# More paired slabs in the feed-forward part, with the down combinations rebuilt from reloaded tiles and adding DMAs

## Chip, cores and metric

The kernel runs on one core of a Trainium2 chip. The metric is the device time of one execution in microseconds (us). Data and results are fp32; every large product is made of three fp32r matmuls (high x high, high x low, low x high parts), so each weight tile and each feature tile is split into a rounded high part and the rest, its low part.

## The reference, cut to what matters

One encoder layer for 256 rows of width 2048. Mixers and cross-attention come first; the change touches only the last part, the feed-forward block.

```
def swiglu(h, w_gate_up, w_down):
    gate, up = jnp.split(h @ w_gate_up, 2, axis=-1)
    return (jax.nn.silu(gate) * up) @ w_down
...
        x = x + swiglu(rms_norm(x, norm_g[l, 2]), w_gate_up[l], w_down[l])
    return rms_norm(x, final_norm_g)
```

`w_gate_up` is 2048 x 11264, `w_down` is 5632 x 2048. The 256 rows are two row blocks of 128.

## The kernel before

**The stream of weights.** All weights lie in one array of slabs of 128 x 2048 (16 blocks of 128 x 128, in the order of use). A slab is loaded by SyncE (SP) into a `raw` buffer. `Stream._half` splits it in halves of 1024 columns: ScalarE (ACT) casts to `wh` (L135), VectorE (DVE) subtracts to `wl` (L136). Four `wh`/`wl` buffers of each kind exist in this part (three, and one of `st.extra`), and `_fill` makes halves ahead as far as they reach. TensorE (PE) takes a half and runs, for each 512 columns and each row block, the three matmuls of `part` (L433, L434, L435; L441 to L443 after the change). A plain slab, "N" in the plans, is 8 such products, 24 matmuls.

**Paired slabs.** A slab marked "S" holds a 2 x 2 set of weight blocks: two feature tiles (`ks`) by two column blocks of 512. With two row blocks it is a product of 2 x 2 block matrices, made with 7 products instead of 8 (Strassen-Winograd), 21 matmuls. It needs sums of weight blocks, which `Stream._sums` makes in four phases of 1024, 512, 1024 and 1024 columns. In the third phase DVE adds 512 columns four times (L157); if the slab is also in `SUMMED`, a DMA that adds (`two`, L102, issued by GpSimd, POOL) has done part of this, and DVE adds twice. Each phase is cast (L159) and subtracted (L160) as above. It also needs combinations of feature tiles, which `combine` makes into a `z` or `y` tile: sums of high and low parts, four sums of 128 columns, then `split2` (L299 on ACT, L283 on DVE) for the high and low parts. In down the fourth piece, x4, goes to half of the first feature's own tile. `forms` names the pieces. The products come in the order 1, b0 (with x4), a0, two of 5 and 7, a1, 6.

**Gate and up.** 11 groups of 512 columns. The first has no pairs. Each of the other ten takes 8 slabs by the plan `GROUP` with 3 S, whose combinations of the 16 features are made once and used in all groups. At the end of a group `mixed`, `gated` and `upped` combine the PSUM banks on DVE and ACT (L1067, L1077), `up` multiplies, transposes (L557) and stores the group's four feature tiles to the `hidden` array (L559, POOL).

**Down.** 44 feature tiles f (k = 0 to 43) by 2048 columns, in two passes of 1024 columns, 22 slabs each by `PASSES`. `fetch` reloads hidden tiles turned (`load_turned`, L564, POOL) and splits them (L291, L283): 22 during gate and up, 22 (`FT - 22` on) at the start of down. Pass 0 begins with four N, which use the features without pairs. `before(j)` makes a combination by hand, if it isn't there yet, when its S comes. Three slabs of the last columns stay for `down_end`, which adds a split of a combined part by a product with the identity (L1244), then the held products of row block 0 and its norm, then of row block 1.

**What sets the order.** `Background` is a list of generators that are stepped between matmuls, by a clock of the program's own (`bg.now`, about one us of PE each) and an account of work that DVE owes. A `yield n` means: not before n us later. `keep_place(mark)` ties each instruction since the mark to the one ahead of it on its engine; where it isn't used, the scheduler of the tile framework may move instructions on their engine. Each engine runs its own in order.

Of the kernel before, what the change touches and what calls it, by code (L numbers as in the profile page):

```python
# [13 lines left out]
F32 = mybir.dt.float32  # L14
F32R = mybir.dt.float32r
# [4 lines left out]
ALU = mybir.AluOpType  # L20
# [3 lines left out]
P = 128  # L24
R = 256
D = 2048
KT = D // P
DFF = 5632
# [15 lines left out]
GATE_UP = 1920 // 16 + 8  # L44
GROUP = "NNSNSNSN"

DOWN = GATE_UP + 80
PASSES = "NNNNSNNSNNSNNSNNSNNSNN", "NSNSNSNSNSNSNSNSNSNNNN"

PAIRED = {a + i for a, plan in [(GATE_UP + 8 * j, GROUP) for j in range(10)] + [(DOWN, PASSES[0]), (DOWN + 22, PASSES[1])]  # L50
          for i, x in enumerate(plan) if x == "S"}
SUMMED = {i for i in PAIRED if i < DOWN}

LAG, OWED, SOON, FAR = 1.3, 0.9, 0.01, 18.0
# [200 lines left out]
class Block:  # L255
# [25 lines left out]
    def tt(self, out, a, b, op):  # L281
        self.bg.dve(math.prod(out.shape[1:]))
        self.nc.vector.tensor_tensor(out=out, in0=a, in1=b, op=op)  # L283
# [14 lines left out]
    def split2(self, hi, lo, src):  # L298
        self.nc.scalar.copy(hi, src)  # L299
        self.tt(lo, src, hi.bitcast(F32), ALU.subtract)  # L300

    def gap(self, pool, n):

        pool.tile([P, n // 4], F32, name=f"gap{next(self.kept)}")
# [132 lines left out]

    def combine(self, z, a, b):

        tt, t, u, v, w = self.tt, *(self.tmp() for _ in range(4))  # L440
        for x, y in ((t, a), (u, b)):  # L441
            tt(x, y[:, 0:R].bitcast(F32), y[:, R:512].bitcast(F32), ALU.add)
        yield SOON  # L443
        tt(v[:, 0:P], t[:, P:R], u[:, P:R], ALU.subtract)
        tt(w[:, 0:P], t[:, 0:P], t[:, P:R], ALU.subtract)
        tt(v[:, P:R], v[:, 0:P], t[:, 0:P], ALU.subtract)
        tt(w[:, P:R], u[:, 0:P], v[:, P:R], ALU.add)
        yield SOON
        hi, lo, x4 = self.forms(z, a)
        self.split2(hi[:, 0:R], lo[:, 0:R], v)  # L450
        if hi.shape[1] == 512:
            self.split2(hi[:, R:512], lo[:, R:512], w)
        else:
            self.split2(hi[:, R:], lo[:, R:], w[:, 0:P])
            self.split2(*x4, w[:, P:R])

# [7 lines left out]
    def paired_rows(self, w, cols, slots, sums, plan, mixed, first, ready=None, late=0, before=None, swap=False):  # L464
# [12 lines left out]
        def put(name, hi, lo, wh, wl):  # L477
            if name not in q:
                for x in [name] if name in count else "1675":
                    q[x] = (self.bank if (name in count) == swap else self.gbank)()  # L480
                    left[x] = count.get(x, s)
            new = left[name] == count.get(name, s)
            left[name] -= 1
            self.part(q[name][:, :], hi, lo, wh, wl, new, left[name] == 0)

        form = lambda t, r: (t[:, r * P:(r + 1) * P], t[:, R + r * P:R + (r + 1) * P])
        n = done = 0
        for i, kind in enumerate(plan):
            if before:
                before(i)  # L490
            if kind == "S":
                ks, z = next(todo)
# [554 lines left out]
    def gate_up(self, gp, f, z):  # L1047
# [39 lines left out]
        def fetch(k0, k1, ahead, pause, wait=0):  # L1087

            m = {}
            for k in range(k0, k1 + ahead):  # L1090
                if k < k1:
                    while len(stored) <= k // 4:
                        yield
                    m[k] = self.tmp()
                    self.load_turned(m[k], self.ff, k)
                if k >= k0 + ahead:
                    while wait and self.bg.now < stored[(k - ahead) // 4] + wait:
                        yield
                    mark = self.mark()
                    self.split(f[k - ahead], m.pop(k - ahead))  # L1100
                    self.keep_place(mark)
                    self.have = k - ahead + 1
                    yield pause
# [18 lines left out]

        sums = [((2 * i, 2 * i + 1), z[i]) for i in range(GROUP.count("S"))]
        comb = self.bg.add(combined())
# [8 lines left out]
        for j in range(1, DFF // 512):  # L1133
            upped(j, self.paired_rows("w_gate_up", [j * 512, DFF + j * 512], self.h3, sums, GROUP, mixed, gated, swap=j % 2 == 0)[0])
        self.bg.drain(early)
        self.fetch = self.bg.add(fetch(FT - 22, FT, 6, SOON))

    def down(self, f, sp):
# [72 lines left out]
    def down_end(self, f, ss, ps, rest, split):  # L1211
# [28 lines left out]

        mark = self.mark()
        for j, parts in split:
            for a in parts:
                nc.tensor.matmul(ps[1][:, j:j + R], self.identr, a, start=False, stop=False)  # L1244
        self.keep_place(mark)
        held = [(k, *st.take("w_down", k, 3 * 512, 4)) for k in rest]
# [644 lines left out]
```

## Time and profile before

| | |
|---|---|
| three runs | 1436.64, 1436.71, 1439.13 us (median 1436.71) |
| profiled execution | 1435.07 us, of it the span from first to last instruction 1433.3 us |
| granted TensorE clock, mean | 0.999 |
| PE, DVE, ACT, POOL busy | 99%, 80%, 57%, 16% |
| DMA, mean over the span | 240 GB/s |

Gate and up with pairs begin near 780 us, down near 1193 us. A row of a timeline has start, length, engine, line, operation, tiles written and read, and in brackets the engine's idle time before it with what ended it. A row of the groups has the count, busy us and mean ns of one, then idle time. The rows themselves are shown where the prediction uses them.

### The profile page before, as it was taken

To read this page: it belongs to the slowest core of one execution; us is meant where nothing else is said; L and a number is where in the kernel's file an instruction comes from. 1 tells how busy PE (TensorE), PEld (TensorE's weight loads), DVE (VectorE), ACT (ScalarE), POOL (GpSimd) and SP (SyncE) were. 2 spreads that over 40 slices of the span, in tenths; PEclk is the share of its full clock that TensorE was granted. 3 is DMA by queue.
4 is the path that set the end of the run, shared out by engine and by line. 5 is a ranking of instruction groups with operands and counts; after the bars stand their busy time and mean duration, and the time that the engine had idled before them with its cause. 6 is when DMAs were issued, how large, how long until landed. Compare 5 with 4: busy or idle time off the path is not lost.

```text
span 1433.3 us, 18652 instructions
## 1 busy us (share of the span) xinstructions
PE 1423.0 (99%) x6589; PEld 1180.7 (82%) x6589; DVE 1146.2 (80%) x1738; ACT 815.2 (57%) x1183; POOL 234.8 (16%) x306
## 2 busy tenths in 40 slices
PE   9999999999999999999999999999999999999997
PEld 8888888888888888888888888888888888888886
DVE  6667868777877767777677888898888888989997
ACT  7556565446645555556554656555555556655655
POOL 0000100013212223531431121122011002000000
PEclk9999999999999999999999999999999999999999
DMA  9876564546667788964986999889999887655554
GB/s 352 299 285 248 205 206 162 175 169 224 202 196 236 234 267 252 274 200 166 289 239 209 286 286 277 278 275 282 294 293 288 268 260 229 219 230 179 193 218 147
DMA packets 73037, 343.79 MB, mean 240 GB/s; under 512 B 10957, under 2 KB 12654, under 8 KB 45168
## 3 DMA queue, kind: packets, MB, share of 16 engines
q1 hardware_dynamic: 54848, 288.98, 57.5%
q0 software_dynamic: 17664, 52.97, 15.8%
q8 instruction: 51, 0.84, 0.2%
q10 hardware_dynamic: 432, 0.66, 0.1%
q14 instruction: 42, 0.34, 0.1%
HBM read 322.12 MB, written 20.45 MB: 239 GB/s over the span
## 4 chain that ended last, share of the span: by engine, by line
PE 97%; DVE 1%; ACT 0%; DMA 0%; issue 0%; SPq 0%; ACTq 0%
PE pg L433 22%; PE pg L434 22%; PE pg L435 22%; PE pm L434 7%; PE pm L435 7%; PE pm L433 7%; PE pg L381 4%; PE pg L382 2%; PE pm L1344 1%; PE pm L1022 1%; PE pm L993 1%; DMA raw<-in_W 0%; PE pm L1753 0%; DVE res L283 0%; PE pm L994 0%
## 5 line engine op out<-in xcount | busy, mean ns | idle before, releaser
L136 DVE TENSOR_TENSOR wl<-raw,wh 128x1024 fp32r<-128x1024 f32 (+1 forms) x413 | 494.8, 1212 | 166.1 <-ACT wh L135 163.2
L135 ACT CAST wh<-raw 128x1024 fp32r<-128x1024 f32 (+1 forms) x413 | 424.5, 1043 | 283.9 <-PE pg L435 196.4
L433 PE MATMUL pg<-wh,act 128*128 128x512 f32 (+1 forms) x1191 | 465.6, 391 | 0.0
L434 PE MATMUL pg<-wl,act 128*128 128x512 f32 (+1 forms) x1191 | 463.9, 389 | 0.4 <-DVE wl L136 0.2
L435 PE MATMUL pg<-wh,act 128*128 128x512 f32 (+1 forms) x1191 | 463.9, 389 | 0.0
L433 PEld LDWEIGHTS pg<-wh,act 128*128 128x128 f32 x1191 | 223.8, 188 | 47.8 <-issue 1.5
L434 PEld LDWEIGHTS pg<-wl,act 128*128 128x128 f32 x1191 | 223.8, 188 | 47.2 <-DVE wl L136 1.3
L435 PEld LDWEIGHTS pg<-wh,act 128*128 128x128 f32 x1191 | 223.7, 188 | 47.2 <-DVE act L283 0.4
L159 ACT CAST wh<-raw 128x1024 fp32r<-128x1024 f32 (+1 forms) x150 | 137.0, 921 | 146.8 <-DVE raw L157 46.4
L160 DVE TENSOR_TENSOR wl<-raw,wh 128x1024 fp32r<-128x1024 f32 (+1 forms) x150 | 156.1, 1061 | 57.0 <-ACT wh L159 56.8
L434 PE MATMUL pm<-wl,act 128*128 128x512 f32 x309 | 120.5, 390 | 0.1
L433 PE MATMUL pm<-wh,act 128*128 128x512 f32 x309 | 120.2, 389 | 0.0
L435 PE MATMUL pm<-wh,act 128*128 128x512 f32 x309 | 120.2, 389 | 0.0
L381 PE MATMUL pg<-act,wh 128*128 128x512 f32 x256 | 90.5, 395 | 0.0
L382 PE MATMUL pg<-act,wl 128*128 128x256 f32 x256 | 71.8, 280 | 0.0
L434 PEld LDWEIGHTS pm<-wl,act 128*128 128x128 f32 x309 | 58.0, 188 | 13.0 <-DVE wl L136 0.6
L433 PEld LDWEIGHTS pm<-wh,act 128*128 128x128 f32 x309 | 58.0, 188 | 12.0
L435 PEld LDWEIGHTS pm<-wh,act 128*128 128x128 f32 x309 | 58.0, 188 | 12.0
L102 POOL DMA_DIRECT2D two<-in_W x30 | 26.6, 887 | 241.2 <-DMA two<-in_W 116.0
L157 DVE TENSOR_TENSOR raw<-raw 128x512 f32<-128x512 f32 x90 | 62.0, 689 | 1.3
L159 ACT CAST wh<-two 128x1024 fp32r<-128x1024 f32 x30 | 31.6, 1052 | 51.1 <-PE pg L435 21.7
L381 PEld LDWEIGHTS pg<-act,wh 128*128 128x128 f32 x256 | 48.1, 188 | 10.5
(375 smaller groups left out, 1821.9 us busy)
## 6 DMA issues: line engine op xcount, KB each, us to landing
raw<-in_W SPq DMA_DIRECT2D x216, 1024.0 KB, 5.6
raw<-in_W SPq DMA_DIRECT2D x30, 768.0 KB, 6.1
two<-in_W SPq DMA_DIRECT2D x60, 256.0 KB, 4.9
two<-in_W POOLq DMA_DIRECT2D x30, 512.0 KB, 9.3
raw<-in_W SPq DMA_DIRECT2D x11, 512.0 KB, 7.6
hidden<-g POOLq DMA_DIRECT2D x22, 256.0 KB, 3.7
tmp<-hidden POOLq DMA_DIRECT2D x44, 128.0 KB, 5.4
features<-tmp POOLq DMA_DIRECT2D x32, 128.0 KB, 5.3
```

The costliest lines, as they stand in the source:

```text
L102: nc.gpsimd.dma_start(t, W[:, 512:1536], accum_op=ALU.add)
L135: nc.scalar.copy(wh[:, a:b], r[:, a:b])
L136: nc.vector.tensor_tensor(out=wl[:, a:b], in0=r[:, a:b], in1=wh[:, a:b].bitcast(F32), op=ALU.subtract)
L157: nc.vector.tensor_tensor(out=out, in0=a, in1=b, op=ALU.add)
L159: nc.scalar.copy(wh, src)
L160: nc.vector.tensor_tensor(out=wl, in0=src, in1=wh.bitcast(F32), op=ALU.subtract)
L381: self.nc.tensor.matmul(p[:, :], wh, slot[:, :], start=start, stop=False)
L382: self.nc.tensor.matmul(p[:, 0:R], wl, slot[:, 0:R], start=False, stop=stop)
L433: self.nc.tensor.matmul(p, hi, wh, start=start, stop=False)
L434: self.nc.tensor.matmul(p, hi, wl, start=False, stop=False)
L435: self.nc.tensor.matmul(p, lo, wh, start=False, stop=stop)
L993: nc.tensor.matmul(p[:, :], q[d][:, r * P:(r + 1) * P], kt[d][:, :], start=d == 0, stop=False)
```

## The change

1. `GROUPS` replaces `GROUP`: every second gate and up group has the plan "NSNSsNSN". Its fourth pair uses a new tile z3; "s" is paired, but not summed by DMA.
2. The down plans have 8 and 10 S in place of 6 and 9.
3. A down combination (`src` given) loads the two features again from `hidden`, in place of adding their high and low parts, and yields 8, 4 and 6 us.
4. `split_far`: the high part by a cast (L305 of the new kernel), the low part as the negated source, written by ACT (L306) to fp32r, to which a DMA from POOL adds the source (L308). It is used in the down combinations and for the last 22 features.
5. `put` keeps the place of its matmuls.
6. The identity products of `down_end` move behind row block 0's held products and norm.

```
-GROUP = "NNSNSNSN"
+GROUPS = "NNSNSNSN", "NSNSsNSN"
...
-PASSES = "NNNNSNNSNNSNNSNNSNNSNN", "NSNSNSNSNSNSNSNSNSNNNN"
+PASSES = "NNNNSNSNSNNSNSNSNNSNSN", "NSNSNSNSSNSNSNSNSSNNNN"
...
+    def split_far(self, hi, lo, src):
+
+        mark = self.mark()
+        self.nc.scalar.copy(hi, src)
+        self.nc.scalar.mul(lo, src, -1.0)
+        self.keep_place(mark)
+        self.nc.gpsimd.dma_start(lo, src, accum_op=ALU.add)
...
-    def combine(self, z, a, b):
+    def combine(self, z, a, b, src=None):
 
         tt, t, u, v, w = self.tt, *(self.tmp() for _ in range(4))
-        for x, y in ((t, a), (u, b)):
-            tt(x, y[:, 0:R].bitcast(F32), y[:, R:512].bitcast(F32), ALU.add)
-        yield SOON
+        if src:
+            for x, k in zip((t, u), src):
+                self.load_turned(x, self.ff, k)
+            yield 8.0
+        else:
+            for x, y in ((t, a), (u, b)):
+                tt(x, y[:, 0:R].bitcast(F32), y[:, R:512].bitcast(F32), ALU.add)
+            yield SOON
...
-        yield SOON
+        yield 4.0 if src else SOON
         hi, lo, x4 = self.forms(z, a)
-        self.split2(hi[:, 0:R], lo[:, 0:R], v)
+        split = self.split_far if src else self.split2
+        split(hi[:, 0:R], lo[:, 0:R], v)
...
+            mark = self.mark()
             self.part(q[name][:, :], hi, lo, wh, wl, new, left[name] == 0)
+            self.keep_place(mark)
...
-                    self.split(f[k - ahead], m.pop(k - ahead))
-                    self.keep_place(mark)
+                    t, x = f[k - ahead], m.pop(k - ahead)
+                    if k0:
+                        self.split_far(t[:, 0:R], t[:, R:512], x)
+                    else:
+                        self.split(t, x)
+                        self.keep_place(mark)
...
-                yield from self.combine(x, *(f[k] for k in ks))
+                yield from self.combine(x, *(f[k] for k in ks), ks)
+                yield 6.0
                 made.append(x)
-                yield 2.0
...
-        mark = self.mark()
-        for j, parts in split:
-            for a in parts:
-                nc.tensor.matmul(ps[1][:, j:j + R], self.identr, a, start=False, stop=False)
-        self.keep_place(mark)
...
         for r in range(2):
+            mark = self.mark()
+            for j, parts in split if r else ():
+                for a in parts:
+                    nc.tensor.matmul(ps[1][:, j:j + R], self.identr, a, start=False, stop=False)
             for k, wh, wl in held:
                 self.part_rows(ps[r], r, f[k], wh, wl, False, k == FT - 1)
+            self.keep_place(mark)
             norm(ps[r], r)
```

More of the change, by code (lines that the diff above doesn't have):

```diff
@@ L44 @@
 GATE_UP = 1920 // 16 + 8
-GROUP = "NNSNSNSN"
+GROUPS = "NNSNSNSN", "NSNSsNSN"
 DOWN = GATE_UP + 80
-PASSES = "NNNNSNNSNNSNNSNNSNNSNN", "NSNSNSNSNSNSNSNSNSNNNN"
-PAIRED = {a + i for a, plan in [(GATE_UP + 8 * j, GROUP) for j in range(10)] + [(DOWN, PASSES[0]), (DOWN + 22, PASSES[1])]
-          for i, x in enumerate(plan) if x == "S"}
-SUMMED = {i for i in PAIRED if i < DOWN}
+PASSES = "NNNNSNSNSNNSNSNSNNSNSN", "NSNSNSNSSNSNSNSNSSNNNN"
+PAIRED = {a + i for a, plan in [(GATE_UP + 8 * j, GROUPS[j % len(GROUPS)]) for j in range(10)] + [(DOWN, PASSES[0]), (DOWN + 22, PASSES[1])]
+          for i, x in enumerate(plan) if x in "Ss"}
+SUMMED = {GATE_UP + 8 * j + i for j in range(10) for i, x in enumerate(GROUPS[j % len(GROUPS)]) if x == "S"}
 LAG, OWED, SOON, FAR = 1.3, 0.9, 0.01, 18.0
@@ L447, in combine @@
         tt(w[:, P:R], u[:, 0:P], v[:, P:R], ALU.add)
-        yield SOON
+        yield 4.0 if src else SOON
         hi, lo, x4 = self.forms(z, a)
-        self.split2(hi[:, 0:R], lo[:, 0:R], v)
+        split = self.split_far if src else self.split2
+        split(hi[:, 0:R], lo[:, 0:R], v)
         if hi.shape[1] == 512:
-            self.split2(hi[:, R:512], lo[:, R:512], w)
+            split(hi[:, R:512], lo[:, R:512], w)
         else:
-            self.split2(hi[:, R:], lo[:, R:], w[:, 0:P])
-            self.split2(*x4, w[:, P:R])
+            split(hi[:, R:], lo[:, R:], w[:, 0:P])
+            split(*x4, w[:, P:R])
     def forms(self, z, a):
@@ L490, in paired_rows @@
                 before(i)
-            if kind == "S":
+            if kind in "Ss":
                 ks, z = next(todo)
@@ L1121, in combined @@
                 yield from self.combine(z, *(self.h3[k] for k in ks))
-        sums = [((2 * i, 2 * i + 1), z[i]) for i in range(GROUP.count("S"))]
+        z = z + [gp.tile([P, 1024], F32R, name="z3")]
+        sums = [((2 * i, 2 * i + 1), z[i]) for i in range(4)]
         comb = self.bg.add(combined())
@@ L1133, in gate_up @@
         for j in range(1, DFF // 512):
-            upped(j, self.paired_rows("w_gate_up", [j * 512, DFF + j * 512], self.h3, sums, GROUP, mixed, gated, swap=j % 2 == 0)[0])
+            plan = GROUPS[(j - 1) % len(GROUPS)]
+            upped(j, self.paired_rows("w_gate_up", [j * 512, DFF + j * 512], self.h3, sums[:8 - plan.count("N")], plan, mixed, gated,
+                                      swap=j % 2 == 0)[0])
         self.bg.drain(early)
```

## The prediction

> **What bounds the kernel now.** I read the page first: the span, the busy shares and the chain that ended last.
>
> ```profile
> span 1433.3 us, 18652 instructions
> ...
> PE 1423.0 (99%) x6589; PEld 1180.7 (82%) x6589; DVE 1146.2 (80%) x1738; ACT 815.2 (57%) x1183; POOL 234.8 (16%) x306
> ...
> PE 97%; DVE 1%; ACT 0%; DMA 0%; issue 0%; SPq 0%; ACTq 0%
> ```
>
> TensorE (PE) is the chain: 97% of it. Removing a matmul shortens the kernel, as long as everything that feeds PE still comes in time. What a matmul is worth is not the 0.39 us that a record lasts, since records overlap; it is the step from one start to the next. From the timeline of PE, the first and the last of a run of 60 matmuls that follow each other:
>
> ```profile
> 1179.71 0.39 PE L434 MATMUL pm<-wl,act 128*128 128x512 f32 x1
> ...
> 1193.08 0.39 PE L433 MATMUL pg<-wh,f 128*128 128x512 f32 x1
> ```
>
> 13.37 us over 59 steps: 0.2267 us each. So a plain slab ("N", 24 matmuls) is 5.44 us of PE and a paired slab ("S", 21) is 4.76 us.
>
> Then I asked how near the other engines are, stretch by stretch (columns: PE, PEld, DVE, ACT, POOL busy, clock, DMA share, GB/s):
>
> ```profile
> 800.00:900.00 100.00, 100.00 (x443) 82.84 (x442) 87.32 (x103) 58.28 (x70) 17.24 (x20) 1.00 0.95 287
> 1200.00:1300.00 100.00, 99.97 (x439) 81.53 (x438) 91.05 (x150) 59.94 (x91) 11.46 (x13) 1.00 0.64 218
> ```
>
> VectorE (DVE) has 87% in the gate and up part and 91% in the down part. It is the second bound, and an S slab is dearer for it than an N slab. So the question is whether DVE and the new DMAs keep PE fed.
>
> The prices, from the groups by form and from the DMA issues (us from issue to landing, last column):
>
> ```profile
> L136 DVE TENSOR_TENSOR wl<-raw,wh 128x1024 fp32r<-128x1024 f32 x408 | 492.0, 1220 | 163.5 <-ACT wh L135 160.6
> L157 DVE TENSOR_TENSOR raw<-raw 128x512 f32<-128x512 f32 x90 | 62.0, 689 | 1.3
> L160 DVE TENSOR_TENSOR wl<-raw,wh 128x512 fp32r<-128x512 f32 x45 | 30.8, 685 | 0.3 <-ACT wh L159 0.3
> L283 DVE TENSOR_TENSOR z<-tmp,z 128x256 fp32r<-128x256 f32 x12 | 4.8, 419 | 0.0
> L299 ACT CAST y<-tmp 128x256 fp32r<-128x256 f32 x9 | 3.6, 403 | 6.3 <-DVE tmp L283 6.3
> L299 ACT CAST y<-tmp 128x128 fp32r<-128x128 f32 x9 | 2.7, 295 | 2.4 <-DVE tmp L283 2.4
> L787 ACT ACTIVATE tmp<-res 128x256 f32<-128x256 f32 x8 | 3.1, 420 | 2.7 <-DVE res L283 2.7
> L564 POOL DMA_DIRECT2D tmp<-hidden x44 | 38.8, 889 | 53.7 <-issue 24.4 <-DMA hidden<-g 13.3 <-DVE act L283 10.0
> L918 POOL DMA_DIRECT2D mr<-values x16 | 8.8, 552 | 30.4 <-DVE kt L283 20.3 <-DVE tmp L1007 9.8 <-issue 0.2
> ```
>
> ```profile
> two<-in_W POOLq DMA_DIRECT2D x30, 512.0 KB, 9.3
> tmp<-hidden POOLq DMA_DIRECT2D x44, 128.0 KB, 5.4
> values<-tmp POOLq DMA_DIRECT2D x16, 128.0 KB, 2.2
> mr<-values POOLq DMA_DIRECT2D x16, 128.0 KB, 3.4
> ```
>
> **What it removes.** Five gate and up groups get a fourth S, pass 0 of down goes from 6 to 8, pass 1 from 9 to 10: 8 S in place of N, 3 matmuls each, 24 x 0.2267 = 5.4 us of PE. On DVE a down combination loses two sums and its three low parts, and 22 late features lose theirs (0.42 us for 128x256). That DVE time was hidden beside PE and is worth nothing by itself.
>
> **The fourth S of the gate and up groups.** An N costs DVE two subtractions of 1.22 = 2.4 us. The new S ("s") is not summed by DMA: three subtractions of 1.22, one of 0.69, four sums of 0.69 = 7.1 us, beside 4.76 us of PE. By the window, a group of 41.5 us (5 N and 3 S) has 0.873 x 41.5 = 36.2 us of DVE; with s in place of an N it is 40.9, and PE's time falls to 40.8. On average DVE is then full in every second group, so each unevenness inside such a group ends on PE. Two places are uneven.
>
> First, the group's opening. The DVE work that ends the group before runs into the next one; from the timeline, DVE and below it the PE matmuls that first use a half:
>
> ```profile
> 860.75 1.22 DVE L136 TENSOR_TENSOR wl<-raw,wh 128x1024 fp32r<-128x1024 f32 x1
> ...
> 865.00 1.30 DVE L557 STREAM_TRANSPOSE g<-h 128x512 f32<-128x512 f32 x2
> 866.23 1.18 DVE L136 TENSOR_TENSOR wl<-raw,wh 128x1024 fp32r<-128x1024 f32 x1
> ```
>
> ```profile
> 867.68 0.39 PE L434 MATMUL pg<-wl,act 128*128 128x512 f32 x1
> 868.36 0.39 PE L434 MATMUL pg<-wl,act 128*128 128x512 f32 x1
> ...
> 869.72 0.39 PE L434 MATMUL pg<-wl,act 128*128 128x512 f32 x1
> ```
>
> Here DVE is free of the old group at 866.23, with an N on PE. In the changed plan ("NS...") an S stands there, and its second, third and fourth phases are first used at 867.68, 868.36 and 869.72. DVE still has to do from 866.23 on: 512 subtraction, sum, 1024 subtraction (third phase, ready at 868.65: 0.3 late), sum, a subtraction of the next N that the built program's order puts ahead, then the fourth phase, ready at 871.6: 1.55 later still. 1.85 us in all.
>
> Second, s follows an S directly. An unsummed S between N slabs, in the down part of before:
>
> ```profile
> 1330.34 1.82 DVE L160 TENSOR_TENSOR wl<-raw,wh 128x1024 fp32r<-128x1024 f32 x2
> ...
> 1335.36 1.22 DVE L160 TENSOR_TENSOR wl<-raw,wh 128x1024 fp32r<-128x1024 f32 x1
> ...
> 1338.26 2.36 DVE L136 TENSOR_TENSOR wl<-raw,wh 128x1024 fp32r<-128x1024 f32 x2
> ```
>
> ```profile
> 1335.80 0.39 PE L434 MATMUL pg<-wl,act 128*128 128x512 f32 x1
> ...
> 1337.84 0.39 PE L434 MATMUL pg<-wl,y 128*128 128x512 f32 x1
> ...
> 1340.56 0.39 PE L434 MATMUL pm<-wl,act 128*128 128x512 f32 x1
> ```
>
> Its first phase is ready 4.2 us ahead (1331.6 for 1335.80) and four sums eat that down to 1.3 us (1336.58 for 1337.84). But whatever follows an S starts only 1.08 us ahead (1339.48 for 1340.56). So s loses 3.1 us of lead, less some 0.7 us of small work that stood between: it is late by about 1.0 us in the third phase, and 0.95 more in the fourth, again behind a subtraction of the next N. 1.95 us. The new z3 is made once, in the first group, which has no S to feed; it costs nothing. Five groups: 5 x 3.8 = 19.0 us. I bound this at 9 us (half) and 28 us (half as much again). In down the same happens at the first adjacent pair of pass 1 (1.95 us), and pass 1 starts one N nearer to the work that ends pass 0 (about 2.4 us, by the same walk): 4.4 us.
>
> **The low parts by DMA.** Before, a combination's low part was one DVE instruction. Now it is a cast and a negation on ScalarE (ACT), an issue on POOL and a landing, three times for each S of down, and the piece that is first needed (x4) is issued last. Two things fix it late. All ten combinations are issued by hand against the S that uses them; with the new 8, 4 and 6 us pauses one takes some 19 us of the program's own clock, and S slabs come every 10 to 16. And both ACT's split and PE's matmuls now hold their order, so PE can't go on with another product. In the built program's order ACT's six instructions stand behind the cast for the third phase of the very S. How late that cast is, from before, with the start of its S below:
>
> ```profile
> 1228.26 1.05 ACT L159 CAST wh<-raw 128x1024 fp32r<-128x1024 f32 x1 [1.78 <-DVE raw L157]
> ```
>
> ```profile
> 1230.48 0.39 PE L433 MATMUL pm<-wh,act 128*128 128x512 f32 x1
> ```
>
> It ends 1.2 us before S; with less DVE work it can come about 0.5 earlier, no more, since it needs a buffer that PE frees. Six instructions (0.40, 0.42, then four of about 0.30, overlapping a little) take 1.9 us: the last ends near S + 0.25. The first use of x4's low part is PE's sixth matmul, S + 1.1. No row shows an accumulation of 64 or 128 KB inside SBUF. Its landing lies between 2.0 us (a little under values<-tmp) and 5.4 (tmp<-hidden); two<-in_W accumulates, but four times the bytes. I take 3.4, from mr<-values, the same shape into SBUF. Landing at S + 3.65: 2.5 us of waiting for each of six S, 15 us.
>
> The other four are worse. At the first S of pass 0 the adds too stand at its door, behind the subtraction of its own fourth phase, which ends near S + 2.6; adds to 3.2, ACT to 5.3, landing 8.7, needed at 1.1: 7.6 us. (POOL is full by then: 16 low parts of 0.55, 13 loads of 0.89 and two stores since the start of down, some 22 us of issues in the 21.8 us that PE takes to the first S.) At the second and third the split stands among those of the features, and a load or a low part goes ahead on POOL: last issue near S + 2.1 and 1.8, waits of 4.4 and 4.1. The last of pass 1 follows another S directly and its split starts near S + 1.4, behind a cast: 5.6. Four features (act 22, 23, 2, 3) are issued some 3 us before use, landing included 0.4 late each: 1.5. Sum 15 + 21.7 + 1.5 = 38 us. With 2.0 for the landing, ten waits are 1.4 shorter and the features don't wait: 22. With 5.4, ten are 2.0 longer and four features 1.0: 62.
>
> [...]
>
> **The end.** The identity matmuls now stand behind row block 0's held products; before, PE's weight loads waited there for the split parts:
>
> ```profile
> 1410.47 0.19 PEld L1244 LDWEIGHTS pm<-tmp,identr 128*128 128x128 f32 x1 [0.20 <-ACT tmp L299]
> ...
> 1410.93 0.19 PEld L1244 LDWEIGHTS pm<-tmp,identr 128*128 128x128 f32 x1 [0.27 <-DVE tmp L283]
> ```
>
> I count these 0.4 us as gained.
>
> **Sum**, on the profiled execution (span 1433.3, time 1435.07; the median of the three runs is 1.64 higher): -5.4 + 19.0 + 4.4 + 38 - 0.4 = +55.6, so 1490.7 there and 1492 as a median.
>
> **Rivals.** (a) The forecast: DVE and DMA both hold PE, 1492; 0.50. (b) The low parts land in time and only DVE is late: -5.4 + 23.4 - 0.4, 1454. For it: the 2.2 us row. Against: even that lands after S + 1.1. 0.12. (c) Only the DMAs cost, because DVE has idle time ahead of each tight place: -5.4 + 38 - 0.4, 1469. For it: before shows leads of 1 us held without loss. Against: that lead is just what s uses up. 0.18. (d) Faster: the split reaches POOL early enough, the other 5.4 us are gained, 1431. That needs ACT to start the six instructions 3 us earlier than now (the last issue by S - 2.3), and DVE to lose none of its leads; one step on the wrong side and it's gone. 0.04, and 0.02 for no change. (e) The waits cost more than themselves, because PE's clock falls after them. The trace shows such a fall behind the last matmul (clock: the third column from the right):
>
> ```profile
> 1428.00:1430.00 2.00, 0.00 (x0) 0.00 (x0) 0.00 (x0) 0.00 (x0) 0.00 (x0) 0.83 1.03 377
> 1430.00:1433.00 3.00, 0.00 (x0) 0.00 (x0) 0.00 (x0) 0.00 (x0) 0.00 (x0) 0.50 0.22 74
> ```
>
> ```profile
> 1424.47 0.24 PE pm L435
> ```
>
> The last row is the last matmul, from the chain. 0.83 is 0.68 us at half clock in 2: the clock fell at 1429.3, some 4.5 us after the last matmul. Two of my waits are longer, two as long. If half clock lasts another 4.5 us, each costs 2.2 us more: 4 to 9 us, 1496 to 1501; with landings of 5.4 us nearly every S would do it, up to 1535. 0.14. [...]
>
> **Numbers.** About 0.2% is what a measurement of this kernel can tell from no change. Faster 0.04, same 0.02, slower 0.94. The range holds (a), (b), (c) and most of (e): 1452 to 1522.
>
> **What would show it.** PE's timeline should have steps of 2 to 6 us inside each S of down, on the third matmul of the second product (act, then f), released by a DMA; in every second gate and up group two steps of 0.5 to 1.6 us, released by DVE. DVE's share in 800 to 1100 us should rise above 90%, and POOL should be full for some 20 us at the start of down. If PE's steps stay at 0.23 us throughout, I am wrong; if only one of the two kinds shows, (b) or (c) holds.

## The result and the profile after

The changed kernel takes 1561.46 us (median of five runs, 1556.29 to 1563.36) against 1436.64 (1435.42 to 1439.13): 1.0863 times as long, 95% interval 1.084 to 1.0885. It is slower, as forecast, but by 125 us and not by 56; 1561 lies outside the range of 1452 to 1522.

The page of the changed kernel: span, busy shares, and the chain that ended last.

```profile
span 1559.1 us, 18804 instructions
...
PE 1459.1 (94%) x6565; PEld 1191.8 (76%) x6565; DVE 1169.5 (75%) x1731; ACT 845.6 (54%) x1256; POOL 300.1 (19%) x378
...
issue 10%; PE 3%; DVE 2%; POOL 2%; DMA 1%; ACT 0%; POOLq 0%; DVEq 0%
```

24 matmuls fewer (6565 against 6589), and yet 36 us more PE busy time: records last longer, above all where the clock is halved (0.63 us each in the rows of S 5 below, against 0.39). The chain that was 97% PE is broken, so it can't be used for shares any more. What tells are PE's groups with idle time ahead of them (line, engine, operation, tiles, count; busy, mean ns; idle before, and what ended it). L441, L442 and L443 are a product's first, second and third matmul (hi by wh, hi by wl, lo by wh):

```profile
L441 PE MATMUL pg<-wh,act 128*128 128x512 f32 (+1 forms) x1196 | 469.7, 393 | 5.4 <-ACT act L305 5.4
L443 PE MATMUL pg<-wh,act 128*128 128x512 f32 (+1 forms) x1196 | 469.4, 393 | 25.9 <-DMA act<-tmp 25.9
...
L442 PE MATMUL pm<-wl,act 128*128 128x512 f32 x279 | 111.3, 399 | 10.9 <-DVE wl L160 10.9
...
L442 PE MATMUL pg<-wl,z 128*128 128x512 f32 x99 | 41.3, 417 | 7.7 <-DVE wl L160 7.7
L443 PE MATMUL pg<-wh,z 128*128 128x512 f32 x99 | 41.1, 415 | 12.0 <-DMA z<-tmp 12.0
...
L443 PE MATMUL pg<-wh,f 128*128 128x512 f32 x42 | 18.5, 441 | 10.5 <-DMA f<-tmp 10.5
...
L443 PE MATMUL pm<-wh,f 128*128 128x512 f32 x30 | 13.0, 432 | 9.6 <-DMA f<-tmp 9.6
```

25.9 + 12.0 + 10.5 + 9.6 = 58.0 us of waiting on the adding DMAs, all at the third matmul, the one that reads a low part; z here is also the tile of the first late features. The second matmul, which reads a weight's low half, waits on VectorE (DVE).

One S of pass 0, the fifth, shows all of it. First POOL's timeline, then PE's (start, duration, engine, line; idle before it in brackets):

```profile
1351.60 1.72 POOL L308 DMA_DIRECT2D y<-tmp  x2 [10.72 <-ACT y L306]
1352.67 1.52 POOL L308 DMA_DIRECT2D f<-tmp  x1
```

```profile
1355.75 0.79 PE L443 MATMUL pg<-wh,f 128*128 128x512 f32 x1 [2.82 <-DMA f<-tmp]
1356.34 0.63 PE L441 MATMUL pg<-wh,f 128*128 128x512 f32 x1
1356.77 0.63 PE L442 MATMUL pg<-wl,f 128*128 128x512 f32 x1
1357.19 0.63 PE L443 MATMUL pg<-wh,f 128*128 128x512 f32 x1
1357.62 0.63 PE L441 MATMUL pm<-wh,y 128*128 128x512 f32 x1
1358.05 0.63 PE L442 MATMUL pm<-wl,y 128*128 128x512 f32 x1
```

POOL idles until ACT has split the pieces, issues the two of y and last the one that PE needs first; PE idles 2.82 us; and behind that its starts lie 0.427 us apart and not 0.227. PE's clock does fall between matmuls: 0.50 was granted from 1355.2 to 1358.5 us. "Half clock" below means such steps.

From PE's timeline of 817 us on I summed, over all matmuls, the step from the start before less 0.2267 us. Steps over 0.62 us are waits, those of 0.40 to 0.62 are put down as half clock:

| place | forecast, us | measured, us |
|---|---|---|
| gate and up | 19.0 | 35.0 |
| four late features, on their DMA | 1.5 | 17.6 |
| S 1 to 3 of pass 0 | 7.6 + 4.4 + 4.1 | 7.8 + 8.7 + 8.2 |
| S 4 to 8 of pass 0 | 5 x 2.5 | 2.6, 3.0, 2.7, 2.5, 2.9 |
| S 9 and 10 | 2.5 + 5.6 | 6.7 + 6.2 |
| pass 1, opening and adjacent pair | 4.4 | 3.9 |
| end | -0.4 | 1.1 |
| half clock in down | 0 (rival e: 4 to 9) | 22.0 |
| small steps in down | 0 | 2.6 |

The right column adds up to 133.5; less the 1.8 that before has in the same stretch and less 5.4 for the matmuls, it is 126.3, and the spans differ by 125.8. Not every wait is one for DVE or for a DMA. Of the 35.0 in gate and up, 22.9 are waits for DVE's weight halves, 3.3 waits for ACT's casts of them, and 8.8 steps below 0.62 us, short waits and half clock. In S 1, 2 and 10, 4.1, 1.6 and 3.0 us are waits for ACT's cast of x4; the first expectations below counted the 4.1 with the features.

The table says where PE lost time, not yet what would give it back. That took the experiments.

### The profile page after: what moved, and what is told of

The parts are those of the page before. It is cut to its first block, busy times and chain, and to the rows that moved or that the text cites. A ratio compares the mean times of both kernels' runs of the same rounds, so it can differ in the third digit from the quotient of the medians.

```text
span 1559.1 us, 18804 instructions
## 1 busy us (share of the span) xinstructions
PE 1459.1 (94%) x6565; PEld 1191.8 (76%) x6565; DVE 1169.5 (75%) x1731; ACT 845.6 (54%) x1256; POOL 300.1 (19%) x378
## 5 line engine op out<-in xcount | busy, mean ns | idle before, releaser
L136 DVE TENSOR_TENSOR wl<-raw,wh 128x1024 fp32r<-128x1024 f32 (+1 forms) x397 | 477.0, 1212 | 196.1 <-ACT wh L135 194.0
L135 ACT CAST wh<-raw 128x1024 fp32r<-128x1024 f32 (+1 forms) x397 | 409.7, 1042 | 329.7 <-PE pg L443 204.1
L443 PE MATMUL pg<-wh,act 128*128 128x512 f32 (+1 forms) x1196 | 469.4, 393 | 25.9 <-DMA act<-tmp 25.9
L441 PE MATMUL pg<-wh,act 128*128 128x512 f32 (+1 forms) x1196 | 469.7, 393 | 5.4 <-ACT act L305 5.4
L442 PE MATMUL pg<-wl,act 128*128 128x512 f32 (+1 forms) x1196 | 468.0, 391 | 0.0
L443 PEld LDWEIGHTS pg<-wh,act 128*128 128x128 f32 x1196 | 226.1, 189 | 76.5 <-DMA act<-tmp 29.1
L159 ACT CAST wh<-raw 128x1024 fp32r<-128x1024 f32 (+1 forms) x182 | 167.0, 923 | 197.5 <-PE pg L443 78.3
L441 PEld LDWEIGHTS pg<-wh,act 128*128 128x128 f32 x1196 | 226.3, 189 | 53.9 <-ACT act L305 6.3
L442 PEld LDWEIGHTS pg<-wl,act 128*128 128x128 f32 x1196 | 226.1, 189 | 47.3 <-DVE wl L136 1.0
L160 DVE TENSOR_TENSOR wl<-raw,wh 128x1024 fp32r<-128x1024 f32 (+1 forms) x182 | 190.3, 1064 | 82.8 <-ACT wh L159 82.7
L442 PE MATMUL pm<-wl,act 128*128 128x512 f32 x279 | 111.3, 399 | 10.9 <-DVE wl L160 10.9
L441 PE MATMUL pm<-wh,act 128*128 128x512 f32 x279 | 110.2, 395 | 1.3 <-ACT wh L159 1.3
L443 PE MATMUL pm<-wh,act 128*128 128x512 f32 x279 | 109.7, 393 | 0.0
L157 DVE TENSOR_TENSOR raw<-raw 128x512 f32<-128x512 f32 x122 | 84.0, 689 | 2.6
L580 POOL DMA_DIRECT2D tmp<-hidden x64 | 69.1, 1129 | 86.1 <-DVE f L283 16.2
L442 PEld LDWEIGHTS pm<-wl,act 128*128 128x128 f32 x279 | 53.0, 190 | 27.3 <-DVE wl L160 16.2
L441 PEld LDWEIGHTS pm<-wh,act 128*128 128x128 f32 x279 | 53.0, 190 | 14.6 <-ACT wh L159 3.5
L443 PEld LDWEIGHTS pm<-wh,act 128*128 128x128 f32 x279 | 53.0, 190 | 10.7
L159 ACT CAST wh<-two 128x1024 fp32r<-128x1024 f32 x30 | 31.4, 1047 | 49.4 <-PE pg L443 27.2
```

The costliest lines, as they stand in the source:

```text
L135: nc.scalar.copy(wh[:, a:b], r[:, a:b])
L136: nc.vector.tensor_tensor(out=wl[:, a:b], in0=r[:, a:b], in1=wh[:, a:b].bitcast(F32), op=ALU.subtract)
L157: nc.vector.tensor_tensor(out=out, in0=a, in1=b, op=ALU.add)
L159: nc.scalar.copy(wh, src)
L160: nc.vector.tensor_tensor(out=wl, in0=src, in1=wh.bitcast(F32), op=ALU.subtract)
L441: self.nc.tensor.matmul(p, hi, wh, start=start, stop=False)
```

## The experiments

Unless said otherwise the comparisons are of three rounds beside runs of the kernel before on the same chip; "saves" is against 1561.5. The kernel before had medians of 1436.2 to 1437.7 in these rounds, so a difference of 2 us between two versions says little.

**All low parts on DVE.**

```
     def split_far(self, hi, lo, src):
...
-        self.nc.scalar.copy(hi, src)
-        self.nc.scalar.mul(lo, src, -1.0)
...
-        self.nc.gpsimd.dma_start(lo, src, accum_op=ALU.add)
+        self.split2(hi, lo, src)
```

> All of the change, but every low part is again one subtraction on VectorE (cast, then subtract) in place of a cast, a negation and an adding DMA. In the changed kernel's trace PE's steps above 0.2267 us in the down part add up so: 21.7 us at the first features, 34.3 at the S slabs of pass 0, 12.9 at the last two S slabs of pass 1, and 22.1 of matmuls at half clock behind these. Theory A (the adding DMAs cause all of that): 1561.5 - 91.0 = 1470. Theory B (VectorE is so full that the low parts, put back on it, are late themselves; 18 combinations of 0.8 us and 22 features of 0.42 us are 24 us of VectorE): 1480 to 1495.

1481.8 us, ratio 1.0311 (1.0296 to 1.0326). It saves 79.7: the adding DMAs are the larger cause. The time lies in theory B's range, at its lower end, but not quite for B's reason: PE's waits in down, 13.7 us with the end's, are all for weight halves, from DVE or from ACT's casts of them, and none is for a low part of a feature or of a combination.

**Old gate and up plan.**

```
-GROUPS = "NNSNSNSN", "NSNSsNSN"
+GROUPS = "NNSNSNSN", "NNSNSNSN"
```

> All of the change but the fourth pair: every gate and up group keeps the plan NNSNSNSN. In the changed kernel's trace PE's steps in gate and up carry 35.0 us above 0.2267 each. Theory A (these 35.0 belong to the fourth pair alone, and the down part does not depend on it): 1561.5 - 35.0 + 3.4 (15 matmuls back) = 1530. Theory B (my price of 19.0 for the fourth pair was right, and the other 16 come from elsewhere): 1546.

1530.1, ratio 1.0649 (1.0633 to 1.0665): theory A to the microsecond. In this kernel the 35 us belong to the fourth pair.

**The fourth pair alone, on the kernel before** (GROUPS, SUMMED, z3 and the choice of the plan; nothing else).

> The kernel before with the fourth pair in every second gate and up group and nothing else of the change. Theory A (the 35.0 us of PE's steps in gate and up belong to it): 1436.6 - 3.4 + 35.0 = 1468. Theory B (the prediction's price of 19.0): 1452.

1457.65, ratio 1.0141 (1.0126 to 1.0157): +20.0, with the 3.4 that its matmuls save 23.4 us of lost time. Neither 35 nor 19, but close to the forecast's term. So something else in the change raises its price from 23 to 35.

**Features' low parts on DVE.**

```
-                    if k0:
+                    if False:
                         self.split_far(t[:, 0:R], t[:, R:512], x)
```

> All of the change, but the 22 late features get their low part from VectorE again; the combinations keep the adding DMAs. Theory A (the features' adding DMAs cost only their own waits, 21.7 us, and 7.1 us of half clock behind them): 1561.5 - 28.8 = 1533. Theory B (they also fill GpSimd's queue and hold the ring of temporary tiles, so that the first three S slabs of pass 0, which waited 7.3, 1.7 and 8.4 us, fall to the 2.9 of the later ones, with some half clock): 1518 to 1524.

1533.1, ratio 1.0673 (1.0655 to 1.0691): theory A; 28.4 us are the late features' own.

**PE's order free.**

```
-            mark = self.mark()
             self.part(q[name][:, :], hi, lo, wh, wl, new, left[name] == 0)
-            self.keep_place(mark)
```

> All of the change, but PE's matmuls are no longer held in the order in which the slabs are written down (the two lines around the call in put are gone); the scheduler may move them past one that waits, as in the kernel before. The fourth pair cost 31.5 us in the changed kernel (1561.5 against 1530.1 without it) and 20.0 alone on the kernel before. Theory A (the 11.5 between them are the price of the held order): 1550, or less where the order also helps the down part. Theory B (the fourth pair is dearer there for another reason): 1561.

1527.2, ratio 1.0623 (1.0606 to 1.0641). It saves 34.3, far more than the 11.5 that I had put down to it: holding PE's order also costs in the down part. By PE's steps 11.3 of it lie in gate and up and 22.2 in down.

**The fourth pair with the order held, on the kernel before** (the same three lines, put in).

> The kernel before with the fourth pair and with PE's matmuls held in the written order, nothing else of the change. Theory A (the held order costs the 11.5 us between the fourth pair's two prices): 1457.7 + 11.5 = 1469. Theory B (it costs nothing without the adding DMAs): 1458.

1466.9, ratio 1.021 (1.0195 to 1.0226): theory A. PE's groups from 817 to 1225 us, first with free order (the fourth pair alone), then held:

```profile
L434 PE MATMUL pm<-wl,act 128*128 128x512 f32 x212 | 83.5, 394 | 2.6 <-DVE wl L160 2.2
...
L434 PE MATMUL pg<-wl,z 128*128 128x512 f32 x72 | 29.0, 403 | 3.4 <-DVE wl L160 3.4
```

```profile
L434 PE MATMUL pm<-wl,act 128*128 128x512 f32 x212 | 85.1, 401 | 10.3 <-DVE wl L160 10.3
...
L434 PE MATMUL pg<-wl,z 128*128 128x512 f32 x72 | 29.6, 411 | 7.6 <-DVE wl L160 7.5
```

The same late halves; with a free order the scheduler puts a hi-by-wh matmul of the next product ahead of the one that waits (37 times in this stretch), and less is left to wait for.

**The held order alone, on the kernel before** (five rounds).

> The kernel before with PE's matmuls held in the written order, and nothing else. Theory A (the order costs only where an operand is late; the kernel before has almost no waits): 1436 to 1438. Theory B (the scheduler's free order also hides small waits of the old plan): 1440 to 1447.

1439.55, ratio 1.0019 (1.001 to 1.0028): +3.0, between the two. Alone it is cheap. 30.7 for pair and order together, 20.0 and 3.0 for each: 7.7 us come only where both meet.

**Shorter pauses.**

```
-            yield 8.0
+            yield 6.0
...
-        yield 4.0 if src else SOON
+        yield 2.0 if src else SOON
...
-                yield 6.0
+                yield SOON
```

These are the pauses after the reload, after the sums and after the split; the old gate and up plan and the features on DVE go with them.

> The change with the old gate and up plan and with VectorE's low parts for the features; the combinations keep the reload and the adding DMAs, but their pauses are 6, 2 and 0.01 us in place of 8, 4 and 6, so that one takes some 8 us of the program's clock and not 18, and gets ahead of the S slabs, which come every 10 to 16 us. With the old pauses the two other edits would give 1561.5 - 31.5 - 28.4 = 1502. Theory A (the S slabs wait because each combination is issued only at its S; made earlier, the landing is hidden): their waits of some 46 us and most of the half clock go, 1440 to 1450. Theory B (the adding DMAs or GpSimd's queue are too slow to be hidden at any place): 1480 to 1500.

1499.65, ratio 1.0437 (1.0421 to 1.0452): 2 us under the sum of the two other edits. The time fits theory B, but POOL's timeline shows that the test did not take place. From S 5 on, each issue still waits for ACT at its S:

```profile
1295.52 1.73 POOL L308 DMA_DIRECT2D y<-tmp  x2 [10.69 <-ACT y L306]
...
1308.81 1.73 POOL L308 DMA_DIRECT2D y<-tmp  x2 [10.70 <-ACT y L306]
```

At S 5 the last piece is issued 1.0 us behind the start of S, in this run as in the changed kernel. The pauses had not moved ACT's part there, so this run could not tell A from B.

**Combinations three slabs ahead, by hand.**

```
-                while plan[j] == "S" and len(made) <= plan[:j].count("S"):
+                while len(made) < plan[:j + 4].count("S"):
```

> The changed kernel with each combination issued three slabs ahead of its S slab and not at its door; nothing else differs. With shorter pauses alone the ScalarE part still stood at the S, behind the cast of its third phase, and the waits of 2.7 to 3.2 us stayed. Theory A (the place in ScalarE's order makes every S late): the ten S waits, 46 us, go, and most of the half clock behind them: 1501 to 1515. Theory B (only the S slabs after the crowded start of down gain, S 4 to 10 with 26.6 us; S 1 to 3 stay held by the late temporary tiles and loads): 1535. Theory C (earlier adds and casts push VectorE's and ScalarE's weight work back): 1550 or more.

1522.6, ratio 1.0594 (1.0574 to 1.0614). It saves 38.8. In PE's groups from 1300 us on one waits for a DMA, where the changed kernel has three (act 15.7, f 10.5 and 9.6 us):

```profile
L443 PE MATMUL pg<-wh,act 128*128 128x512 f32 x54 | 23.0, 425 | 6.7 <-DMA act<-tmp 6.7
...
L443 PE MATMUL pg<-wh,f 128*128 128x512 f32 x30 | 12.2, 405 | 0.0
...
L443 PE MATMUL pm<-wh,f 128*128 128x512 f32 x30 | 11.7, 389 | 0.0
```

The two rows of f, which carried S 5 to 10, wait for nothing now, and in PE's timeline no S of down waits for a piece any more. So the landing can be hidden, and the place of the combination, ACT's split with it, made the S slabs late; the edit moves loads and sums too, so it does not part ACT from these. The time lies below B and above A for another reason than B's: the waits at the first late features grew from 17.6 to 33.0 us, and in POOL's timeline the combinations' pieces now stand among theirs.

**The piece needed first, first.**

```
+        if hi.shape[1] != 512:
+            split(*x4, w[:, P:R])
         split(hi[:, 0:R], lo[:, 0:R], v)
...
-            split(*x4, w[:, P:R])
```

> The changed kernel with the three pieces of a combination split in another order: the 128-column one that the second product needs is cast, negated and issued first and not last. In the changed kernel's trace the issues of one combination lie 0.6 us apart and ScalarE takes 0.96 us for the other two pieces. Theory A (the wait in an S is this queue and one landing of 2.8 us): the S waits at issue time, ten of them, fall by 1.0 to 1.2 us each, with some half clock: 1545 to 1552. Theory B (the landing alone counts, or the other pieces are then late, which are needed 0.7 us and more behind): 1558 to 1561.

1548.4, ratio 1.0781 (1.0762 to 1.08): theory A, 13 us. POOL and PE at the same S as above:

```profile
1348.65 0.85 POOL L308 DMA_DIRECT2D f<-tmp  x1 [13.10 <-ACT f L306]
1349.26 1.98 POOL L308 DMA_DIRECT2D y<-tmp  x2
```

```profile
1351.05 0.50 PE L443 MATMUL pg<-wh,f 128*128 128x512 f32 x1 [0.38 <-DMA f<-tmp]
```

0.38 us of waiting in place of 2.82. The other pieces are then late in S 3, 4 and 9, which takes part of it back.

**Features loaded 3 ahead, not 6.**

```
-        self.fetch = self.bg.add(fetch(FT - 22, FT, 6, SOON))
+        self.fetch = self.bg.add(fetch(FT - 22, FT, 3, SOON))
```

> The changed kernel with the late features loaded 3 ahead and not 6, so that half as many temporary tiles wait for their adding DMA. Theory A (the ring of 11 tiles is what stalls GpSimd's queue at the start of down): the waits at the features, 23 us, fall by half, and with them S 1 to 3: 1540 to 1550. Theory B (what counts there is the landing of 8 us beside stores and weight loads): the waits stay or grow by the shorter lead, 1561 to 1575.

1559.65, ratio 1.0856 (1.0833 to 1.0879): no difference, so the ring of temporary tiles is not what holds the first features. The reading of POOL's waits behind theory A was wrong.

**Adding DMAs for the features alone.**

```
-        split = self.split_far if src else self.split2
+        split = self.split2
```

> The changed kernel with adding DMAs for the 22 late features alone; the combinations keep their reload, but get their low parts from VectorE. All low parts on VectorE took 1481.8. Theory A (the features' waits of 8.3 and 4.4 us and those behind them come from their own DMAs, in a stretch in which the DMA engines are 95% busy): 1481.8 + 28.4 = 1510, or at least 1481.8 + 12 + 5 of half clock = 1499. Theory B (they come from the combinations' DMAs in the same queue): 1482 to 1487.

1511.0, ratio 1.0516 (1.0496 to 1.0536): theory A. PE's group of z, 1225 to 1300 us, with no adding DMA of a combination about:

```profile
L443 PE MATMUL pg<-wh,z 128*128 128x512 f32 x12 | 6.3, 527 | 11.3 <-DMA z<-tmp 11.3
```

What is special there are the landings. The views of the tiles z (1225 to 1260 us) and y (all of it) in the changed kernel, and its windows (PE, PEld, DVE, ACT, POOL busy, clock, DMA share, GB/s):

```profile
DMA to landing us min/median/max: 2.7/8.3/10.1
```

```profile
DMA to landing us min/median/max: 2.6/2.8/7.2
```

```profile
1230.00:1243.00 13.00, 5.08 (x22) 3.90 (x21) 4.59 (x4) 4.45 (x10) 6.61 (x8) 0.85 0.95 261
...
1338.00:1343.00 5.00, 2.55 (x11) 1.80 (x10) 2.72 (x6) 1.72 (x5) 2.71 (x3) 1.00 0.53 77
```

The same DMA of 128 KB lands in 2.7 us alone and in 8.3 among the last stores, the features' loads and the weights, with the 16 DMA engines 95% busy; before, DVE needed 0.42 us there.

Is it POOL's own queue that is full, or the 16 engines? S 9 tells. Its combination issues the same three pieces as those of S 5 to 8. These are the DMAs whose issue falls into 1501.3 to 1508 us in the changed kernel, the last two pieces and one weight slab from SP:

```profile
raw<-in_W SPq DMA_DIRECT2D x1, 1024.0 KB, 5.3
y<-tmp POOLq DMA_DIRECT2D x1, 64.0 KB, 3.7
f<-tmp POOLq DMA_DIRECT2D x1, 64.0 KB, 6.7
```

The piece f, which lands in 3.0 to 3.1 us in S 5 to 8, takes 6.7 here, with no store and no feature load about. What differs in the rows is the slab: it is issued 1.6 us behind f, and 1.05 MB of SP's queue move before f lands. In S 5 to 8 a slab comes 1.7 to 2.0 us behind f, and 0.02 to 0.12 MB of it move by then. So POOL's queue alone, which holds the same three pieces, does not make f late. Why so much of the slab went first here, these rows do not show.

**Does the half clock cost time of its own?** The waits of pass 0's S slabs were filled with matmuls of a zero tile, first all eight, then (five rounds) the last four. `fill` is the number for that S; the tile `zero` is made once.

```
         self.nc.tensor.matmul(p, hi, wl, start=False, stop=False)
+        for _ in range(fill):
+            self.nc.tensor.matmul(p, self.zero, wh, start=False, stop=False)
         self.nc.tensor.matmul(p, lo, wh, start=False, stop=stop)
```

> The changed kernel with matmuls of an all-zero tile put into PE's wait at each S slab of pass 0 (14, 28, 33, 9, 11, 10, 9, 11 of them, about as long as the waits of 3.9, 7.3, 8.4, 2.8, 3.2, 3.0, 2.7 and 3.1 us); they add zero to the sum and take no time that is not waited out. Theory A (PE's clock falls because it stood idle in the wait): the matmuls behind those waits run at 0.227 us a step and not 0.427, some 8 to 10 us less, 1552. Theory B (the clock is low in this stretch for another reason): 1561, or a few us more where a filler is longer than its wait.

> The changed kernel with matmuls of an all-zero tile in the waits of the last four S slabs of pass 0 alone (11, 10, 9 and 11 of them, 2.0 to 2.5 us in waits of 2.7 to 3.2 us); they add zero. Behind these four the trace has 23 matmuls at 0.43 us and not 0.227, 4.6 us. Theory A (half clock costs what it lasts where nothing else is late): 1561.5 - 4.6 = 1557. Theory B (the next wait takes it up, since the data of the next S do not come from PE): 1561.

1562.7, ratio 1.0878 (1.0854 to 1.0901), and 1563.9, ratio 1.0886 (1.0868 to 1.0905): no gain in either. The clock does answer; 1340 to 1400 us, the changed kernel and then the one with the last four filled:

```profile
1340.00:1360.00 20.00, 14.74 (x58) 11.77 (x59) 13.00 (x15) 9.52 (x15) 3.48 (x5) 0.91 0.64 182
1360.00:1380.00 20.00, 17.43 (x77) 14.11 (x76) 13.76 (x16) 10.49 (x16) 2.60 (x3) 1.00 0.66 206
1380.00:1400.00 20.00, 17.65 (x71) 14.10 (x70) 12.98 (x15) 10.34 (x21) 3.54 (x5) 0.91 0.45 136
```

```profile
1340.00:1360.00 20.00, 17.34 (x75) 13.58 (x74) 12.49 (x16) 10.46 (x21) 5.97 (x7) 1.00 0.60 156
1360.00:1380.00 20.00, 19.61 (x86) 15.73 (x85) 13.81 (x14) 11.70 (x17) 2.61 (x3) 1.00 0.62 192
1380.00:1400.00 20.00, 19.76 (x87) 15.93 (x86) 14.38 (x17) 10.07 (x20) 2.62 (x3) 1.00 0.58 185
```

From S 5 to S 6, where the changed kernel has seven slow matmuls, the period falls from 14.38 to 13.31 us, most of their 1.4; but at S 8 the step behind its fillers is 4.0 us, in both runs, where the changed kernel had 3.1 without any, and the gain is gone. Why S 8 gets later is not shown. That idleness lowers the clock is shown: 0.91 in the first and third of these windows, and 1.00 with the waits filled. What the 22 us of half clock cost by themselves is not: they are an upper bound, and these runs got none of them back.

**Only the new down plans, on the kernel before.**

```
-PASSES = "NNNNSNNSNNSNNSNNSNNSNN", "NSNSNSNSNSNSNSNSNSNNNN"
+PASSES = "NNNNSNSNSNNSNSNSNNSNSN", "NSNSNSNSSNSNSNSNSSNNNN"
```

> The kernel before with 8 and 10 pairs in down, and nothing else: sums and low parts by VectorE as before. Theory A (VectorE, 91% busy in this part, has no room for three more S slabs; 3 x 4.7 us of it more, and the adjacent pair of pass 1 is late as forecast, 4.4 us): 1436.6 - 2.0 + 4.4 to 10 = 1439 to 1445. Theory B (VectorE's idle time takes it up): 1434.6, which a measurement of this kernel tells from before hardly.

1447.5, ratio 1.0078 (1.0061 to 1.0095): +11.4, a little over theory A. The three extra S slabs cost more than the forecast's +2.4 even without a DMA: PE's waits in down are 7.2 us, all for ACT's casts, and steps of half clock add 3.8.

**Two tries for a better down part.** Combinations ahead, features on DVE, free order, old gate and up plan; the second (five rounds) also with the old pass 1 and two slabs ahead.

> The down part of the change at its best, as far as the runs show it: combinations three slabs ahead with the reload and the adding DMAs, features' low parts by VectorE, PE's order free, old gate and up plan, new down plans, identity matmuls moved. Theory A (nothing is left that holds PE but the two places of VectorE in pass 1, some 4 us, less 9 matmuls of 2.0 us and 0.4): 1436 to 1440. Theory B (the features or the first S slabs still wait at the start of down, 7 to 20 us): 1445 to 1458.

> The kernel before with 8 pairs in pass 0 of down only (pass 1 with its old 9), combinations two slabs ahead with the reload and the adding DMAs, features' low parts by VectorE, the identity matmuls moved, PE's order free. With 10 pairs in pass 1 and three slabs ahead the same took 1459, with 5.1 us at a feature behind the first combination, 4.0 at the first S, some 6 in pass 1 and 6 of half clock. Theory A (two slabs ahead leave the first features their place in GpSimd's queue, and the old pass 1 has none of its waits): 1436.2 - 1.4 - 0.4 + 0 to 6 = 1434 to 1441. Theory B (the reloads push the features back as before): 1445 to 1455.

1459.3, ratio 1.0156 (1.014 to 1.0171), and 1454.4, ratio 1.0131 (1.0114 to 1.0148): theory B both times, the first 1 us above its range. The four edits of the first together give back 102.2 of 125; singly they save 31.4, 28.4, 34.3 and 38.8, 133 in all, so they overlap by 31. No version run beats the kernel before.

**The identity matmuls alone** (five rounds; the move, on the kernel before).

> The kernel before with the identity matmuls behind row block 0's held products, and nothing else. Theory A (they had covered the subtraction of the first held slab, which is now waited for, 1.1 us against 0.4 saved): 1436.2 + 0.7 = 1436.9. Theory B (the forecast's term): 1435.8. A measurement tells the two hardly; the step in PE's timeline does.

1437.6, ratio 1.001 (1.0001 to 1.0018), half of the 0.2% that the forecast gave as what can be told from no change. PE's weight load at the first held product shows what is late now:

```profile
1413.45 0.19 PEld L434 LDWEIGHTS pm<-held,act 128*128 128x128 f32 x1 [1.38 <-DVE held L127]
```

The identity matmuls had covered DVE's subtraction of the first held slab. The term is about +1.0 and not -0.4.

## Why the prediction was right, and where it was wrong

The direction and the places were right, the sum was short by 69 us. Three steps make up nearly all of it: the waits at the late features and the S slabs of down (38 in the sum, 68.9 measured), the fourth pair in gate and up (19.0 and 35.0), and the half clock in down, which the sum left out (22.0).

Right: the sign; the kinds of place (third matmul on a DMA in down, second on DVE in gate and up); the price of the fourth pair by itself (19.0 against 23.4 of lost time, bounds 9 to 28); the landing in a quiet stretch (3.4 taken, 2.8 median); the waits of S 1 and of S 4 to 8, which came out at 7.8 and 2.5 to 3.0 for 7.6 and 2.5; pass 1's two places (4.4 against 3.9). In part the 2.5 was luck: at S 5 the last issue came 1.0 us behind the start of S and not 0.25, and the piece landed in 3.0 and not 3.4 us. The step that named ACT's place behind the cast as the cause of the late S holds as far as the runs go: with the combinations three slabs ahead those waits went, and moving the last piece to the front cut 13 us.

Wrong, by size:
- The fourth pair. The place where s follows an S came out as forecast, at 2.0 us in four of the five groups (1.95). The group's opening did not: 2.1 to 4.0 us and not 1.85, 15.4 in all for 9.3. The 8.8 us of shorter steps had no term.
- The step "Two things fix it late" named the held order of PE for the down part, as a reason and without a price. Freeing it gives back 34.3 us: in gate and up some 11 of the 16 us by which the term of 19.0 fell short, the rest in down. This is another cut through the same lost time and does not add to it, since the forecast let each late operand end on PE, as a held order does.
- The term "four features, 1.5". They were issued 2.0 to 3.2 us before use, as forecast; but the landing of 3.4 was carried over from rows of a quieter stretch to the start of down, and there the four landed in 10.1, 7.3, 3.8 and 6.6 us. Measured at PE 17.6, and 28.4 for the edit. The same error is in S 3 (8.2 for 4.1), in S 9 (6.7 for 2.5) and in part in S 2 (8.7 for 4.4), where the last issue also came 1.7 us later than forecast. The bound of 5.4 was the row nearest to it; even that was short for this stretch.
- "POOL should be full for some 20 us at the start of down". It was busy for 6.6 of the 13 us from 1230 us on (the window above) and waited for landings in between, 6.39 us of it for one of z.
- Rival (e), clock falls, was put at 0.14 as a case beside (a). Both hold at once: 22.0 us of half-clock steps, not 4 to 9. I had asked for idle times of more than 4.5 us, from the one fall in before; here the clock was 0.50 behind a wait of 2.35 us at one S. Its share in the time stays open, as the fillers show.
- The down plans: -2.0 + 4.4 forecast, +11.4 measured on the kernel before with the sums still on DVE.
- "DVE's share in 800 to 1100 us should rise above 90%". From 800 to 1180 us, before and then after:

```profile
800.00:1180.00 380.00, 379.94 (x1676) 313.95 (x1675) 329.59 (x389) 215.20 (x251) 61.86 (x72) 1.00 0.92 281
```

```profile
800.00:1180.00 380.00, 364.12 (x1560) 293.05 (x1559) 326.11 (x387) 209.78 (x245) 60.72 (x70) 0.99 0.88 265
```

It went from 87% to 86%. By the forecast's prices the five s give DVE some 23 us more work (an estimate, 7.1 less 2.4 us each), but PE's waits make gate and up some 31 us longer, so the share does not rise. The cost was in the two uneven places, as forecast, but a full DVE was the wrong sign to look for.

Rival (b), only DVE late, and (c), only the DMAs, are out: each half removed leaves the other's cost (+44 us without the adding DMAs, +92 without the fourth pair).

## What to carry to other kernels

Price a DMA by its landing in the very stretch where it will run, not by its median: the same 128 KB took 2.7 and 8.3 us, and a piece of 64 KB took 3.0 and, while a whole weight slab moved, 6.7. An order that is held by hand is nearly free while every operand comes in time (+3.0 us here) and makes every lateness that another edit brings dearer (34 us), so cost it together with that edit. Before you hide a transfer by starting it earlier, look at the engine that releases it: here the pauses were shortened in vain, and only a new place in the written order moved the issue. And look at what is pushed back: the combinations three slabs ahead waited for nothing, and the features beside them waited 15 us more.

## What the runs showed of the hardware

- PE's clock fell in waits between matmuls or just behind them: to 0.50, with steps of 0.427 us for 128x512 in place of 0.227. The length of the wait alone did not decide it: at waits of 2.82, 2.74 and 2.35 us the clock fell, at 2.57 and 2.45 us it did not. What decided it, these five waits do not tell. Windows of the changed kernel, with the columns of those above (PE's busy time third, the clock third from the right): the wait of 2.57 us and the matmuls behind it, then the wait of 2.35 us and matmuls from 1.15 us behind it on.

```profile
1367.56:1370.13 2.57, 0.00 (x2) 0.00 (x1) 1.23 (x1) 0.00 (x0) 1.01 (x2) 1.00 1.03 133
1370.13:1372.30 2.17, 2.17 (x10) 1.79 (x10) 0.51 (x1) 1.59 (x2) 0.00 (x0) 1.00 0.79 313
1386.06:1388.41 2.35, 0.00 (x0) 0.00 (x0) 1.23 (x1) 0.00 (x0) 0.81 (x1) 1.00 0.74 90
1389.56:1391.69 2.13, 2.13 (x7) 1.64 (x5) 1.62 (x2) 1.43 (x2) 0.00 (x0) 0.50 0.91 381
```

- Matmuls of zeros in the waits kept the clock at 1.00 from 1340 to 1400 us, where the changed kernel had 0.91, 1.00 and 0.91 in its three windows.
- An adding DMA inside SBUF: 64 and 128 KB both land in 2.6 to 3.1 us when little else runs, 64 KB in 6.7 us while a weight slab of 1 MB moved, and 128 KB in up to 10.1 us at the start of down, among stores, loads and weights.
